# New states of the sample group updated in place, with five buffers and steps ten weight units apart, in a hybrid recurrent decoder step

## The chip, the cores and the metric

The kernel is one program on one core of a Trainium2 chip. The core has a matrix engine (TensorE, PE), a vector engine (VectorE, DVE), an activation engine (ScalarE, ACT), GpSimd (POOL) and an engine that here only issues transfers (SyncE, SP), and 16 DMA engines between HBM and the on-chip memory. Times are device microseconds (us) of one execution. The measure is the median of several runs.

## The reference: what is computed

One inference step of a decoder layer for 256 prompt tokens and 8 samples that share the weights, 264 columns in all. Three token mixers (RWKV-7, mLSTM, gated linear attention) run between one input projection and one output projection; a SwiGLU block follows. Besides the outputs, the new recurrent states are results. For the 8 samples, one token each, the three updates are (cut from the reference):

```python
S = (S * jnp.exp(ld_t)[:, :, None, :]                                  # RWKV-7, per head 64 x 64
     - jnp.einsum('bhvk,bhk->bhv', S, kk_t)[..., None] * (kk_t * a_t)[:, :, None, :]
     + v_t[..., :, None] * k_t[..., None, :])
C = a_c[..., None, None] * C + jnp.einsum('bhs,bhsd,bhse->bhde', w_s, kc, vc)   # mLSTM, 4 heads 256 x 256
S = jnp.exp(bL[:, :, 0, :])[..., None] * S + jnp.einsum('bhsd,bhse->bhde', kc * jnp.exp(bL - b), vc)  # GLA, 4 heads 128 x 256
gg, uu = jnp.split(rmsnorm(x, norm2_g) @ ffn_w_gu, 2, axis=-1)
x = x + (jax.nn.silu(gg) * uu) @ ffn_w_down
```

With one token, each update is "old state times a decay, plus an outer product of a value and a key".

## The kernel before

**The weight stream.** All matrices are stored as one stream of 613 units, most of them 128 x 1024 elements (512 KB). For each unit `weights` loads `raw` (3 buffers) on SP's queue at line 331, ACT rounds it to `wh` (line 334, 3 buffers), DVE subtracts to get the remainder `wl` (line 257, 3 buffers), and PE multiplies: 24 matmuls of 128 x 264 to a unit, three for each 128 x 128 block (`wh` by the input's high part, `wh` by its low part, `wl` by its high part). A `raw` buffer comes free when `wl` of the unit three before it is written, so one turn of the buffers is three units.

**What goes on beside it.** After the products of each half unit's columns `fill` may run a step of other work. The samples' new states are such work: `later` makes 16 jobs `new_C` (mLSTM, two samples of a head to a job), then 16 jobs `new_S` (GLA), then 8 jobs `new_W` (RWKV-7). They are written in the program from the SwiGLU block on; a scheduler decides where they stand on each engine, and it places them from the output projection on, over units 316 to 408 of the stream.

**A job new_C.** It loads `Cb` (the old state, 512 KB, 3 buffers) and `kb` (the key, spread over all partitions, 256 KB, 2 buffers). ACT makes the outer product in `kv` (four instructions, 2 buffers), DVE adds the scaled old state to it (two instructions), SP stores `kv` to `o_sC`.

**A job new_S.** It loads `Sb` and `kgb` (256 KB each); POOL multiplies `Sb` by the decay in `kgb`, ACT makes the outer product in `kvg` (four instructions, buffers shared with `kv`), DVE adds the two, SP stores `kvg` to `o_sg`.

**A job new_W.** It loads `Ss` (256 KB), works on it in place on POOL and DVE, and stores it to `o_swkv`.

Every engine takes its own instructions in order, and SP too: a transfer whose wait is not over holds those behind it. Stores of the states are issued by SP straight behind the instruction that makes them; other stores go through `store`, a list that the next `fill` issues.

Of the kernel before, what the change touches and what calls it, by code (L numbers as in the profile page):

```python
# [16 lines left out]
P = 128  # L17
T = 256
B = 8
# [7 lines left out]
INV = 28  # half-units that the inverse is given  # L27
CT = 6
LAST = 4  # gates left for the change from the mixers to the widening
# [18 lines left out]
def _groups():  # L48
    """The weight stream in the order of its use: (name, matrix, column ranges of 256 in all, K-tile ranges)."""
# [45 lines left out]
def _feat(v):  # L95
    """(..., 128 * n) -> (128, n, ...)"""
    v = np.asarray(v)
    v = v.reshape(v.shape[:-1] + (-1, P))
    return np.ascontiguousarray(np.moveaxis(np.moveaxis(v, -1, 0), -1, 1))


def _pad_r(v):
    """R columns -> 26 tiles of 128, the last half empty"""
    out = np.zeros(v.shape[:-1] + (26 * P,), np.float32)
    out[..., :3264] = v
    return out
# [89 lines left out]
def _rows(s):  # L196
    """(B, head, k, 256) -> (head, 128, B, 2, k): a state with its values on the partitions"""
# [4 lines left out]
def _cols(s):  # L202
    """back from _rows"""
# [22 lines left out]
def _unfeat(v):  # L226
    """(128, n, m) -> (m, 128 * n)"""
# [20 lines left out]
def body(tc, a, stop=None):  # L248
# [21 lines left out]
    with ctx:  # L270
# [10 lines left out]
        # ---------------------------------------------------------------- constants  # L281
# [34 lines left out]
        # ---------------------------------------------------------------- the weight stream  # L316
# [23 lines left out]
        def unit(name, ps, k0, nk, hi, lo, kof=0, soon=True):  # L340
            """the products of one unit of weights"""
# [17 lines left out]
        def project(name, hi, lo, kof=0):  # L359
            """The two output tiles of a group of the stream, in PSUM."""  # L360
# [10 lines left out]
        def store(out, in_):  # L371
            """issued a step after what it stores, so that the queue of loads doesn't wait for it"""
            stores.append((out, in_))

        def fill():
            """between the products of the stream: a step of the mixers, now and then one of the samples'"""
# [19 lines left out]
        def both(*gens):  # L396
            """generators side by side"""
# [5 lines left out]
        def table(last):  # L403
            """ACT's tables for exp and ln, after the last use of others"""
# [4 lines left out]
        def scaled(dst, ps):  # L409
            """a group's two tiles, each token by its norm"""  # L410
# [10 lines left out]
        def csum(o, w, hl):  # L421
            """o = w^T (hi + lo) for a w that float32r holds exactly"""
# [7 lines left out]
        # ---------------------------------------------------------------- scratch in DRAM  # L430
# [11 lines left out]
        # ---------------------------------------------------------------- input norm  # L442
# [7 lines left out]
        def first(k0, nk):  # L450
            """a chunk of x: split with the norm's weight; what the norm divides by comes after the product"""
# [34 lines left out]
        def setup():  # L486
            """what the mixers need a little later"""
# [7 lines left out]
            # the low-rank factors of RWKV, both parts of a split on top of one another  # L495
# [24 lines left out]
        # what the samples leave for later  # L520
# [15 lines left out]
        # ---------------------------------------------------------------- RWKV-7  # L536
# [9 lines left out]
        def shift(j, p, dst, rows=P):  # L546
            """token shift: dst = p + (prev - p) * mu; the row that the next call needs is kept"""
# [8 lines left out]
        def sigmoid(x):  # L556
            """1 / (1 + e) from e = exp(-z), in place"""
# [3 lines left out]
        def stack(i, x):  # L561
            """a low-rank factor's input, split, each part twice"""
# [29 lines left out]
        def r_pre(sts, p, r, k, v):  # L592
            """everything of a pair of heads up to the products of its chunks"""
# [90 lines left out]
        def r_inverse(q, sts):  # L684
            """(I + N)^-1 of the 16-blocks of two pairs, by back substitution, one block on a partition"""
# [37 lines left out]
        def r_post(st):  # L723
            p, A, Nr, X, XT, UV, PR, QKt, W = (st[n] for n in ("p", "A", "Nr", "X", "XT", "UV", "PR", "QKt", "W"))
            # 16-blocks to 32-blocks
# [19 lines left out]
            # 32-blocks to 64  # L745
# [15 lines left out]
            # the chain of chunks  # L761
# [61 lines left out]
        def pipeline(jobs):  # L823
            """a stage of every job under way, the eldest first, and one more job"""
# [10 lines left out]
        def dot(out, x, y):  # L835
            """rows of x by rows of y"""
# [734 lines left out]
```

## Time and profile before

| | |
|---|---|
| median of 3 runs | 2044.55 us (2038.8 to 2045.91) |
| the profiled execution, first to last instruction (span) | 2041.8 us |
| PE busy | 1975.7 us, 97% of the span |
| DVE, ACT, POOL busy | 1338.4, 1041.5, 166.5 us |
| DMA | 414.89 MB, mean 203 GB/s |

The span runs from the first instruction to the last; no other time of that execution is given, so it is compared with the runs as it stands: 2.75 us under their median, and inside them. "Busy" of PE counts pipelined matmuls that lie over one another; whether PE keeps its pace is read from the number of matmuls that a stretch holds.

### The profile page before, as it was taken

To read this page: it belongs to the slowest core of one execution; us is meant where nothing else is said; L and a number is where in the kernel's file an instruction comes from. 1 tells how busy PE (TensorE), PEld (TensorE's weight loads), DVE (VectorE), ACT (ScalarE), POOL (GpSimd) and SP (SyncE) were. 2 spreads that over 40 slices of the span, in tenths; PEclk is the share of its full clock that TensorE was granted. 3 is DMA by queue.
4 is the path that set the end of the run, shared out by engine and by line. 5 is a ranking of instruction groups with operands and counts; after the bars stand their busy time and mean duration, and the time that the engine had idled before them with its cause. 6 is when DMAs were issued, how large, how long until landed. Compare 5 with 4: busy or idle time off the path is not lost.

```text
span 2041.8 us, 41005 instructions
## 1 busy us (share of the span) xinstructions
PE 1975.7 (97%) x16526; PEld 1924.8 (94%) x16526; DVE 1338.4 (66%) x2382; ACT 1041.5 (51%) x1700; POOL 166.5 (8%) x257
## 2 busy tenths in 40 slices
PE   8899999999999889999999999999999999999997
PEld 7898999999998888989999998889999999999997
DVE  7776776776775788776566666568754455555554
ACT  5855655655654345556433566554443344444443
POOL 5100100100100321110000000023000000000000
PEclk9999999999999999999999999999999999999999
DMA  8553554564563778658777798888655555555564
GB/s 255 178 182 117 172 178 127 168 174 135 171 174 111 232 254 278 215 170 256 227 227 229 257 311 295 296 297 279 217 176 184 178 186 181 182 184 178 179 183 136
DMA packets 173526, 414.89 MB, mean 203 GB/s; under 512 B 47512, under 2 KB 69432, under 8 KB 173336
## 3 DMA queue, kind: packets, MB, share of 16 engines
q1 hardware_dynamic: 172904, 411.53, 63.2%
q8 instruction: 129, 2.11, 0.4%
q10 hardware_dynamic: 432, 0.74, 0.1%
q14 instruction: 61, 0.50, 0.1%
HBM read 379.61 MB, written 32.61 MB: 202 GB/s over the span
## 4 chain that ended last, share of the span: by engine, by line
PE 70%; DMA 11%; DVE 8%; ACT 6%; issue 3%; SPq 1%; POOL 0%; DVEq 0%; ACTq 0%; POOLq 0%
PE ps L266 63%; PE mx L266 6%; DMA o_sC<-kv 4%; DVE wl L257 4%; ACT wh L334 3%; DMA kgb<-rg_d 2%; DMA of<-o_d 1%; DMA raw<-wst 1%; DVE dot L838 1%; DMA Ss<-wkv 1%; ACT kvg L263 0%; ACT sg L263 0%; ACT kv L263 0%; SPq L331 0%; DVE xl L260 0%
## 5 line engine op out<-in xcount | busy, mean ns | idle before, releaser
L257 DVE TENSOR_TENSOR wl<-raw,wh 128x1024 fp32r<-128x1024 f32 (+2 forms) x613 | 749.1, 1224 | 459.7 <-ACT wh L334 455.3
L334 ACT CAST wh<-raw 128x1024 fp32r<-128x1024 f32 (+2 forms) x613 | 632.2, 1033 | 621.7 <-PE ps L266 542.7
L266 PE MATMUL ps<-xh,wh 128*128 128x264 f32 x2080 | 612.8, 295 | 9.9 <-ACT wh L334 9.8
L266 PE MATMUL ps<-xh,wl 128*128 128x264 f32 x2080 | 598.2, 288 | 14.2 <-DVE wl L257 14.1
L266 PE MATMUL ps<-xl,wh 128*128 128x264 f32 x2080 | 597.3, 287 | 0.0
L266 PE MATMUL ps<-gh,wl 128*128 128x264 f32 x1408 | 402.2, 286 | 13.1 <-DVE wl L257 12.9
L266 PEld LDWEIGHTS ps<-xh,wh 128*128 128x128 f32 x2080 | 397.2, 191 | 18.3 <-ACT wh L334 10.5
L266 PEld LDWEIGHTS ps<-xh,wl 128*128 128x128 f32 x2080 | 396.1, 190 | 18.6 <-DVE wl L257 17.6
L266 PE MATMUL ps<-gh,wh 128*128 128x264 f32 x1408 | 400.9, 285 | 1.7 <-ACT wh L334 1.5
L266 PE MATMUL ps<-gl,wh 128*128 128x264 f32 x1408 | 399.5, 284 | 0.0
L266 PEld LDWEIGHTS ps<-xl,wh 128*128 128x128 f32 x2080 | 397.6, 191 | 1.3
L266 PEld LDWEIGHTS ps<-gh,wl 128*128 128x128 f32 x1408 | 264.5, 188 | 18.4 <-DVE wl L257 18.1
L266 PEld LDWEIGHTS ps<-gh,wh 128*128 128x128 f32 x1408 | 265.0, 188 | 2.8 <-ACT wh L334 2.5
L266 PEld LDWEIGHTS ps<-gl,wh 128*128 128x128 f32 x1408 | 265.1, 188 | 0.0
L266 PE MATMUL ps<-al,wh 128*128 128x264 f32 x704 | 200.5, 285 | 0.0
L266 PE MATMUL ps<-ah,wh 128*128 128x264 f32 x704 | 200.2, 284 | 0.0
L266 PE MATMUL ps<-ah,wl 128*128 128x264 f32 x704 | 199.8, 284 | 0.0
L266 PEld LDWEIGHTS ps<-ah,wl 128*128 128x128 f32 x704 | 133.1, 189 | 0.0
L266 PEld LDWEIGHTS ps<-al,wh 128*128 128x128 f32 x704 | 132.2, 188 | 0.0
L266 PEld LDWEIGHTS ps<-ah,wh 128*128 128x128 f32 x704 | 132.2, 188 | 0.0
L266 PE MATMUL ps<-oh,wh 128*128 128x264 f32 x384 | 109.0, 284 | 0.0
L266 PE MATMUL ps<-oh,wl 128*128 128x264 f32 x384 | 109.0, 284 | 0.0
(406 smaller groups left out, 2382.0 us busy)
## 6 DMA issues: line engine op xcount, KB each, us to landing
raw<-wst SPq DMA_DIRECT2D x579, 512.0 KB, 3.5
raw<-wst SPq DMA_DIRECT2D x32, 384.0 KB, 3.2
Ct<-mC SPq DMA_DIRECT2D x16, 512.0 KB, 5.1
Cb<-mC SPq DMA_DIRECT2D x16, 512.0 KB, 6.7
o_sC<-kv SPq DMA_DIRECT2D x16, 512.0 KB, 6.4
g_d<-sgate SPq DMA_DIRECT2D x24, 264.0 KB, 4.3
sgl<-g_d SPq DMA_DIRECT2D x24, 264.0 KB, 4.0
qb<-rq_d SPq DMA_DIRECT2D x4, 1024.0 KB
```

Source lines behind the costliest of these rows:

```text
L257: vec.tensor_tensor(out=out, in0=x, in1=y, op=op)
L266: pe.matmul(out, lhsT=lhsT, rhs=rhs, start=start, stop=stop)
L334: act.copy(out=wh[:, 0:nk, :], in_=raw[:, 0:nk, :])
L838: vec.tensor_tensor_reduce(out=tm[:, 0:x.shape[1]], in0=x, in1=y, scale=1.0, scalar=0.0, op0=MUL, op1=ADD, accum_out=out)
```

## The change

The three updates work in the tile that holds the old state, all three kinds share five buffers (tag `st`), the key tiles have three instead of two, the stores go through the list `store` instead of straight to SP, and `every[0]` goes from 4 to 10, so a step of this work is written after every tenth `fill` instead of every fourth. In `new_C` ACT scales the old state (two instructions of 512 columns) and DVE adds the outer product (four of 256); in `new_S` POOL's product stays, ACT has nothing to do, and DVE adds the outer product (four of 128).

```diff
         def new_C(h, b):
-            Cb = fp.tile([P, 2, 2, 256], F32, name="Cb", bufs=3)
+            Cb = fp.tile([P, 2, 2, 256], F32, tag="st", name="Cb", bufs=5)
             load(Cb, a["mC"][h, :, b:b + 2])
-            kb = fp.tile([P, 2, 256], F32, name="kb", bufs=2)
+            kb = fp.tile([P, 2, 256], F32, tag="kb", name="kb", bufs=3)
             load(kb, row(rk_d, BW * b + 256 * h, [[BW, 2], [1, 256]]))
             yield
-            kv = fp.tile([P, 2, 2, 256], F32, name="kv", bufs=2)
+            for i in range(2):
+                af(Cb[:, i], Cb[:, i], AF.Identity, scale=scS[:, h, b + i:b + i + 1])
+            yield
             for i in range(2):
                 for j in range(2):
-                    af(kv[:, i, j, :], kb[:, i, :], AF.Identity, scale=vS[:, 0, 2 * h + j, b + i:b + i + 1])
-            yield
-            for i in range(2):
-                if i:
-                    yield
-                stt(kv[:, i], Cb[:, i], scS[:, h, b + i:b + i + 1], kv[:, i], MUL, ADD)
-            nc.sync.dma_start(out=a["o_sC"][h, :, b:b + 2], in_=kv)
+                    stt(Cb[:, i, j, :], kb[:, i, :], vS[:, 0, 2 * h + j, b + i:b + i + 1], Cb[:, i, j, :], MUL, ADD)
+            store(a["o_sC"][h, :, b:b + 2], Cb)

         def new_S(h, b):
-            Sb = fp.tile([P, 2, 2, P], F32, name="Sb", bufs=3)
+            Sb = fp.tile([P, 2, 2, P], F32, tag="st", name="Sb", bufs=5)
...
-            kv = fp.tile([P, 2, 2, P], F32, tag="kv", name="kvg", bufs=2)
             pool.tensor_tensor(out=Sb, in0=Sb, in1=kb[:, :, 1:2, :].to_broadcast([P, 2, 2, P]), op=MUL)
+            yield
             for i in range(2):
                 for j in range(2):
-                    af(kv[:, i, j, :], kb[:, i, 0, :], AF.Identity, scale=vS[:, 1, 2 * h + j, b + i:b + i + 1])
-            yield
-            tt(kv, kv, Sb, ADD)
-            nc.sync.dma_start(out=a["o_sg"][h, :, b:b + 2], in_=kv)
+                    stt(Sb[:, i, j, :], kb[:, i, 0, :], vS[:, 1, 2 * h + j, b + i:b + i + 1], Sb[:, i, j, :], MUL, ADD)
+            store(a["o_sg"][h, :, b:b + 2], Sb)

         def new_W(v0):
-            S = fp.tile([P, 8, 64], F32, tag="Sb", name="Ss", bufs=3)
+            S = fp.tile([P, 8, 64], F32, tag="st", name="Ss", bufs=5)
...
-            nc.sync.dma_start(out=a["o_swkv"][:, v0:v0 + 8, :], in_=S)
+            store(a["o_swkv"][:, v0:v0 + 8, :], S)
...
-        every[0] = 4
+        every[0] = 10
...
-        while bg:
+        while bg or stores:
             fill()
```

Where the instructions stand moves less than the number ten suggests: the state loads stand between the same weight units as before (the first `Cb` behind unit 316 in both, the first `Sb` behind 364 and now 366, the last `Ss` behind 403 and now 401).

**First place: SP and ACT, late in the new_C jobs.** SP before; the numbers name tiles, in the order in which they are made:

```order
L331 DMA raw_16287<-wst 128x1024
L369 DMA kb_16819<-rk_d_98 128x2x256
L1469 DMA o_sC<-kv_16740 128x1024
L331 DMA raw_16317<-wst 128x1024
L331 DMA raw_16369<-wst 128x1024
L369 DMA Cb_16899<-mC 128x1024
L331 DMA raw_16399<-wst 128x1024
L369 DMA kb_16901<-rk_d_98 128x2x256
L1469 DMA o_sC<-kv_16812 128x1024
```

and ACT before, at the same place; `kv_16894` takes the buffer that `kv_16740` had:

```order
L334 CAST wh_16246<-raw_16245 128x1024
L263 ACTIVATE kv_16894<-kb_16819,vS_459 128x256
L334 CAST wh_16288<-raw_16287 128x1024
L1527 ACTIVATE sil_16208<-gut_16205 128x264
L263 ACTIVATE kv_16894<-kb_16819,vS_459 128x256 x3
```

SP now:

```order
L331 DMA raw_16267<-wst 128x1024
L369 DMA Cb_18244<-mC 128x1024
L331 DMA raw_16307<-wst 128x1024
L331 DMA raw_16347<-wst 128x1024
L369 DMA kb_18246<-rk_d_98 128x2x256
L379 DMA o_sC<-Cb_17902 128x1024
L331 DMA raw_16378<-wst 128x1024
L369 DMA Cb_18425<-mC 128x1024
```

and ACT now:

```order
L427 CAST ah_15757<-sil_16169 128x264
L334 CAST wh_16268<-raw_16267 128x1024
L263 ACTIVATE Cb_18244<-Cb_18244,scS_458 128x512 x2
L334 CAST wh_16308<-raw_16307 128x1024
L334 CAST wh_16348<-raw_16347 128x1024
```

Before, ACT's `kv_16894` stands ahead of the rounding of `raw_16287`, and it needs the buffer that is stored by a transfer issued behind `raw_16287`. Now ACT's instruction on the state waits for the load `Cb_18244`, issued behind `raw_16267`, and stands behind the rounding of `raw_16267`; in 10 of the 16 jobs one or both of the two stand one unit earlier, as the store's user did before.

**Second place: DVE at the same jobs.** Before:

```order
L257 TENSOR_TENSOR wl_16289<-raw_16287,wh_16288 128x1024
L257 TENSOR_TENSOR sil_16208<-sil_16208,gut_16205 128x264
L260 SCALAR_TENSOR_TENSOR kv_16894<-Cb_16817,scS_458,kv_16894 128x512
L257 TENSOR_TENSOR al_15758<-sil_16208,ah_15757 128x264
L260 SCALAR_TENSOR_TENSOR kv_16894<-Cb_16817,scS_458,kv_16894 128x512
L257 TENSOR_TENSOR wl_16319<-raw_16317,wh_16318 128x1024
L257 TENSOR_TENSOR wl_16371<-raw_16369,wh_16370 128x1024
```

and now:

```order
L257 TENSOR_TENSOR wl_16269<-raw_16267,wh_16268 128x1024
L260 SCALAR_TENSOR_TENSOR Cb_18244<-kb_18246,vS_459,Cb_18244 128x256
L257 TENSOR_TENSOR wl_16309<-raw_16307,wh_16308 128x1024
L260 SCALAR_TENSOR_TENSOR Cb_18244<-kb_18246,vS_459,Cb_18244 128x256 x3
L257 TENSOR_TENSOR wl_16349<-raw_16347,wh_16348 128x1024
```

The load `kb_18246` is issued behind `raw_16347`, and DVE's first use of it now stands ahead of `wl_16309`, the unit before `raw_16347`. That is so in 11 of the 16 jobs; in the other 5 the first use stands behind that unit. Before, it was ACT that used the key: in 10 jobs behind the rounding of the very unit that the load followed, in 6 ahead of it.

**Third place: DVE and SP in the new_S jobs.** SP and DVE before:

```order
L331 DMA raw_17126<-wst 128x1024
L369 DMA Sb_17790<-gS 128x512
L369 DMA kgb_17792<-rg_d_99 128x2x256
L1484 DMA o_sg<-kvg_17784 128x512
L331 DMA raw_17156<-wst 128x1024
```

```order
L257 TENSOR_TENSOR wl_17085<-raw_17083,wh_17084 128x1024
L257 TENSOR_TENSOR kvg_17856<-kvg_17856,Sb_17790 128x512
L257 TENSOR_TENSOR wl_17128<-raw_17126,wh_17127 128x1024
L257 TENSOR_TENSOR wl_17158<-raw_17156,wh_17157 128x1024
L257 TENSOR_TENSOR gut_17116<-ps_16983,rs2_15894 128x264
```

and now:

```order
L331 DMA raw_17001<-wst 128x1024
L369 DMA kgb_19990<-rg_d_99 128x2x256
L379 DMA o_sg<-Sb_19678 128x512
L331 DMA raw_17041<-wst 128x1024
L369 DMA Sb_20140<-gS 128x512
```

```order
L257 TENSOR_TENSOR wl_16963<-raw_16961,wh_16962 128x1024
L260 SCALAR_TENSOR_TENSOR Sb_19988<-kgb_19990,vS_459,Sb_19988 128x128 x4
L257 TENSOR_TENSOR wl_17003<-raw_17001,wh_17002 128x1024
L260 SCALAR_TENSOR_TENSOR Sb_20140<-kgb_20142,vS_459,Sb_20140 128x128 x4
L257 TENSOR_TENSOR wl_17043<-raw_17041,wh_17042 128x1024
```

Both times DVE's use of a job (`kvg_17856` there, `Sb_19988` here) stands ahead of the `wl` of the unit behind which its key is loaded (`raw_17126`, `raw_17001`). The store has moved one unit later.

## Rows read from the trace of the kernel before

**Rows 1.** The page, part 1: busy time, share of the span, instructions.
```profile
PE 1975.7 (97%) x16526; PEld 1924.8 (94%) x16526; DVE 1338.4 (66%) x2382; ACT 1041.5 (51%) x1700; POOL 166.5 (8%) x257
```

**Rows 2.** Busy time by stretch (from:to, length, engines with instruction counts, clock, DMA).
```profile
1140.00:1180.00 40.00, 40.00 (x332) 40.00 (x331) 25.84 (x37) 24.00 (x44) 0.00 (x0) 1.00 0.91 299
1180.00:1305.00 125.00, 117.64 (x927) 113.60 (x926) 81.01 (x113) 74.56 (x133) 0.00 (x0) 1.00 0.90 302
1305.00:1400.00 95.00, 87.99 (x700) 85.35 (x699) 58.75 (x75) 53.99 (x110) 25.57 (x18) 1.00 0.91 297
1400.00:1440.00 40.00, 37.37 (x297) 36.17 (x296) 39.83 (x55) 14.27 (x17) 14.17 (x6) 1.00 0.76 256
```

**Rows 3.** Waits, 1130 to 1440 us: who for whom, total, times, longest.
```profile
ACT kv L263 <- DMA o_sC<-kv: 40.3, 13, 5.2
...
ACT kvg L263 <- DMA kgb<-rg_d: 28.2, 14, 4.3
DVE kvg L257 <- POOL Sb L1478: 26.0, 12, 4.1
...
ACT kv L263 <- DMA kb<-rk_d: 2.6, 2, 2.3
```

**Rows 4.** Timeline of SP, ACT and DVE over one turn of new_C.
```profile
1246.67 0.33 SPq L331 DMA_DIRECT2D raw<-wst  x1
1247.05 0.42 SPq L1469 DMA_DIRECT2D o_sC<-kv  x1
...
1253.59 1.31 ACT L263 ACTIVATE kv<-kb,vS 128x256 f32<-128x256 f32 x3 [4.29 <-DMA o_sC<-kv]
1254.80 1.03 ACT L334 CAST wh<-raw 128x1024 fp32r<-128x1024 f32 x1
...
1255.87 1.23 DVE L257 TENSOR_TENSOR wl<-raw,wh 128x1024 fp32r<-128x1024 f32 x1 [0.58 <-ACT wh L334]
...
1257.12 0.33 SPq L331 DMA_DIRECT2D raw<-wst  x1
```

**Rows 5.** DMA issues, 1140 to 1440 us: size, median us to landing.
```profile
raw<-wst SPq DMA_DIRECT2D x93, 512.0 KB, 5.4
Cb<-mC SPq DMA_DIRECT2D x16, 512.0 KB, 6.7
o_sC<-kv SPq DMA_DIRECT2D x16, 512.0 KB, 6.4
kb<-rk_d SPq DMA_DIRECT2D x16, 256.0 KB, 6.5
```

**Rows 6.** The tile kb: its loads' time to landing.
```profile
DMA to landing us min/median/max: 5.2/6.5/8.9
```

**Rows 7.** DVE's groups by form: busy us, mean ns.
```profile
L260 DVE SCALAR_TENSOR_TENSOR kv<-Cb,scS,kv 128x512 f32<-128x512 f32 x32 | 23.4, 747 | 25.3 <-ACT kv L263 25.2
...
L260 DVE SCALAR_TENSOR_TENSOR o<-o,vecs,bon 128x256 f32<-128x256 f32 x8 | 3.6, 477 | 0.0
...
L260 DVE SCALAR_TENSOR_TENSOR y<-natR,sc,y 128x64 f32<-128x64 f32 x1 | 0.3, 285 | 0.0
```

**Rows 8.** Timeline of SP, POOL and DVE in two new_S jobs.
```profile
1338.44 0.38 SPq L369 DMA_DIRECT2D kgb<-rg_d  x1
...
1339.23 1.29 POOL L1478 TENSOR_TENSOR Sb<-Sb,kgb 128x512 f32<-128x512 f32 x1 [4.17 <-DMA kgb<-rg_d]
...
1341.39 1.23 DVE L257 TENSOR_TENSOR wl<-raw,wh 128x1024 fp32r<-128x1024 f32 x1
...
1344.86 1.29 POOL L1478 TENSOR_TENSOR Sb<-Sb,kgb 128x512 f32<-128x512 f32 x1 [4.33 <-DMA kgb<-rg_d]
...
1346.19 0.69 DVE L257 TENSOR_TENSOR kvg<-kvg,Sb 128x512 f32<-128x512 f32 x1 [3.22 <-POOL Sb L1478]
...
1347.68 1.22 DVE L257 TENSOR_TENSOR wl<-raw,wh 128x1024 fp32r<-128x1024 f32 x1
```

**Rows 9.** SP's own waits, 1130 to 1440 us.
```profile
SPq L369 <- DMA o_swkv<-Ss: 9.9, 5, 2.9
```

More of the change, by code (lines that the diff above doesn't have):

```diff
@@ L1461, in new_C, with new_S @@
+            yield
             for i in range(2):
                 for j in range(2):
-                    af(kv[:, i, j, :], kb[:, i, :], AF.Identity, scale=vS[:, 0, 2 * h + j, b + i:b + i + 1])
+                    stt(Cb[:, i, j, :], kb[:, i, :], vS[:, 0, 2 * h + j, b + i:b + i + 1], Cb[:, i, j, :], MUL, ADD)
+            store(a["o_sC"][h, :, b:b + 2], Cb)
+        def new_S(h, b):
+            Sb = fp.tile([P, 2, 2, P], F32, tag="st", name="Sb", bufs=5)
+            load(Sb, a["gS"][h, :, b:b + 2])
+            kb = fp.tile([P, 2, 2, P], F32, tag="kb", name="kgb", bufs=3)
+            load(kb, row(rg_d, 1536 * b + 384 * h + 128, [[1536, 2], [1, 256]]))
+            yield
+            pool.tensor_tensor(out=Sb, in0=Sb, in1=kb[:, :, 1:2, :].to_broadcast([P, 2, 2, P]), op=MUL)
@@ L1464, in new_C @@
             yield
             for i in range(2):
-                if i:
-                    yield
-                stt(kv[:, i], Cb[:, i], scS[:, h, b + i:b + i + 1], kv[:, i], MUL, ADD)
-            nc.sync.dma_start(out=a["o_sC"][h, :, b:b + 2], in_=kv)
-        def new_S(h, b):
-            Sb = fp.tile([P, 2, 2, P], F32, name="Sb", bufs=3)
-            load(Sb, a["gS"][h, :, b:b + 2])
-            kb = fp.tile([P, 2, 2, P], F32, tag="kb", name="kgb", bufs=2)
-            load(kb, row(rg_d, 1536 * b + 384 * h + 128, [[1536, 2], [1, 256]]))
-            yield
-            kv = fp.tile([P, 2, 2, P], F32, tag="kv", name="kvg", bufs=2)
-            pool.tensor_tensor(out=Sb, in0=Sb, in1=kb[:, :, 1:2, :].to_broadcast([P, 2, 2, P]), op=MUL)
-            for i in range(2):
@@ L1496, in new_W @@
             yield
-            tm = fp.tile([P, 8, 64], F32, tag="kb", name="tms", bufs=2)
+            tm = fp.tile([P, 8, 64], F32, tag="kb", name="tms", bufs=3)
             pool.tensor_tensor(out=tm, in0=along(5), in1=col(uR), op=MUL)
```

## The prediction

> **What bounds the kernel now.** The page comes first. PE is busy for 97% of the span [rows 1], so the only time to be won is where PE loses its pace, and busy time hides that, because matmuls lie over one another. The count of matmuls by stretch shows it. From 1140 to 1180 us there are 332 in 40 us, 0.1205 us each, as in undisturbed stretches; a weight unit of 24 then takes 2.89 us and a turn of the three `raw` buffers 8.67 us. By that pace the 927 matmuls of 1180 to 1305 need 111.7 us of the 125, the 700 of 1305 to 1400 need 84.4 of the 95, and the 297 of 1400 to 1440 need 35.8 of the 40 [rows 2]. So 13.3, 10.6 and 4.2 us are lost, 28 us in all, and these three stretches are the jobs new_C, new_S and new_W. That is 1.4% of the kernel, and more than that the change cannot win. The clock is at its full level in all of them, and the DMA engines are 0.90, 0.91 and 0.76 busy [rows 2].
>
> Next come the waits, which say who makes PE late. ACT stood 40.3 us, 13 times, until a store `o_sC` had landed, 28.2 us for `kgb`, and only 2.6 us for `kb`; DVE stood 26.0 us for POOL's `Sb` [rows 3]. ACT and DVE make `wh` and `wl`, so every such wait stands in front of the weights.
>
> The timeline of one turn shows the loop in new_C. `raw` is issued at 1246.67, the store behind it at 1247.05; ACT may write `kv` again only at 1253.59, then rounds that `raw` at 1254.80, DVE makes `wl` at 1255.87, and that frees the buffer for the `raw` at 1257.12 [rows 4]. One turn took 10.45 us against 8.67. The loss of 1.78, 13 times, would be 23 us; PE lost 13.3, because the weights made ahead absorb the rest. I take that share, 0.57, as what a lengthening of this loop costs PE.
>
> **The change, part by part.**
>
> *new_C, ACT.* The wait for the store goes: no tile is written while its store is under way, unless it is the fifth before. In its place ACT waits for the load `Cb`, at the same depth in 10 of 16 jobs and one unit later in the others, as the order shows. The nearest rows for the two prices are the transfers themselves: the store lands after 6.4 us, the load after 6.7 [rows 5]. So the turn through ACT stays about as long. The Trainium skill (DMA: Bandwidth & Descriptors, section on the anatomy of one DMA) says that the receipt of the write makes most of a transfer's fixed cost, and that HBM as the target is the heaviest case; by it the wait taken away would be longer than the one put in. The rows don't bear that out, since the store into HBM is the shorter by 0.3 us; by the rule new_C would gain, which is a rival below.
>
> *new_C, DVE.* This is new. In 11 of 16 jobs DVE's first use of `kb` stands one unit deeper than the load's own unit, so two `wl` wait for a load that was issued behind the later of their two `raw`. The turn is then: 0.38 from `raw` to the next issue (as 1246.67 to 1247.05), the landing of `kb`, one instruction of 256 columns, a `wl`, three more, a `wl`. A `scalar_tensor_tensor` of 256 columns takes 0.477 us [rows 7], a `wl` 1.23 [rows 4], so it is 0.38 + 0.48 + 1.23 + 1.43 + 1.23 = 4.75 plus the landing. With the median of 6.5 it is 11.25, with the least, 5.2, it is 9.95 [rows 6]. In the other 5 jobs all four stand before one `wl`: 0.38 + 1.91 + 1.23 = 3.5 plus the landing, 10.0 or 8.7. Against 8.67, the 16 jobs cost 11 x 2.58 + 5 x 1.33 = 35 us with the median, and 11 x 1.28 + 0 = 14 with the least. PE's share of 0.57 makes 20 and 8, where 13.3 is lost now: +7 or -5. If nothing is absorbed, the upper end is 35 - 13 = +22. I take the median, since it is this same load behind the same neighbours, and a little off it for a stretch that is less crowded when it is longer: **+6 us**, kept between -5 and +22. The part on ACT runs beside it and isn't added.
>
> *new_C, work.* Two instructions of 512 columns at 0.747 us become four of 256 at 0.477: 1.91 for 1.49 a job [rows 7], 6.6 us of DVE over 16 jobs, already inside the turn. The Trainium skill (VectorE: DVE Perf Modes, section on the TRN2 errata) says that each instruction pays a fixed cost and that tiles of 512 elements or more should be used, which speaks against this cut. Its fixed 58 cycles at 0.96 GHz would be 0.06 us an instruction, an estimate by that page, 2 us over the 32 added ones. The rows agree in direction and make it larger: 2 x 0.477 - 0.747 = 0.21 us.
>
> *new_S.* ACT's four instructions go, and its wait of 28.2 us [rows 3] with them. But DVE waits for POOL at the same depth as before, as the third place in the order shows, and the chain ends on DVE. From POOL's start to the start of `wl` it is now 1341.39 - 1339.23 = 2.16 us, and 1347.68 - 1344.86 = 2.82 in the next job, where other work lies between [rows 8]. Afterwards it is POOL's 1.29 plus four instructions of 128 columns. Between 0.285 for 64 and 0.477 for 256 [rows 7] the straight line gives 0.349, four make 1.40, where `kvg` takes 0.69 [rows 8]. The sum is 2.69, 0.5 longer than the one and 0.1 shorter than the other: on the mean +0.2, 16 times 3.2, PE's share **+2 us**. Bounds: 16 x 0.53 = +8 on one side; on the other, if ACT's wait was the true holder in half of the jobs, half of the 10.6 comes back, -5.
>
> *new_W.* The arithmetic stays. SP's wait of 9.9 us until a store of `Ss` lands [rows 9] goes, since five buffers stand where three stood. But DVE is busy for 39.83 of these 40 us [rows 2], and earlier loads don't shorten that. **-1 us**, between -4.2, all that is lost, and 0.
>
> *Stores a step later, spacing of ten.* The order shows stores zero to two units later and the jobs over the same units; a later store delays no load, as the fifth buffer is still free. Zero, hidden by the `raw` waits that SP has anyway. Were the jobs spread in truth, the DMA share of 0.9 would fall; the order says that they are not.
>
> **The sum.** 6 + 2 - 1 = +7 us on the profiled 2041.8, or 2048.8. The runs' median stands 2.75 above that span, so I forecast **2051 us**, 0.3% slower. Of this kernel a difference of about 0.5%, 10 us, is what a measurement can tell from none; the forecast lies inside it.
>
> **The rivals.**
>
> *Faster: the store was the true holder.* If a load that ACT waits for is there in time, because nothing but a free buffer holds it, the 40.3 us of waits vanish. For it: the store's wait is the longest of all on ACT and `kb` cost ACT only 2.6 us [rows 3]. Against it: the order has the loads no earlier. Three quarters of new_C's loss come back, -10, with -3 each from new_S and new_W: 2044.55 - 16 = 2028.5. This is also how it would go by the Trainium skill's rule on write receipts.
>
> *Slower: the key's load on DVE isn't absorbed.* PE waits for `wl`, and `wl` stands behind `kb` two deep; with the lead used up, the full +22 falls due, and +8 in new_S: 2044.55 + 30 = 2074.5. It decides from a landing of about 6 us at a share near one. For it: the loop is closed in 11 jobs, one after another. Against it: the present loop was not charged in full either.
>
> *No difference: the DMA engines set the pace.* At 0.90 busy [rows 2] the same bytes may need the same time whoever waits: 2044.5. For it, the share; against it, stretches nearly a tenth idle, with waits by turns.
>
> **How the numbers follow.** The forecast, -4 to +14 around 2051, has 0.47, the faster rival 0.20, the slower 0.18, the pace of the DMA 0.15. From 2030 to 2068 about 8 in 10 is held: beyond lie half of the faster rival and a little less than half of the slower. Without the rivals the range is 2040 to 2059. Slower by over 0.5% are most of the slower rival (0.16) and the upper part of the forecast (0.15), 0.31; faster 0.20, nearly all the faster rival; within it 0.49.
>
> **What would show it.** No wait of ACT for `o_sC`; in its place one for `Cb` of some 2 to 3 us a job. DVE waiting for `kb`, 20 us or more in all. Four instructions of 0.48 and 0.35 us. ACT without waits in new_S, DVE's wait for POOL still near 26 us. Some 33 us of PE's pace lost over the three stretches instead of 28. The forecast is wrong if `kb` lands before DVE comes to it, if new_C's turn stays under 9.5 us, or if the lost matmuls are found elsewhere than here.

## The result and the profile after

The changed kernel takes 2051.64 us in the median of 6 runs (2048.97 to 2055.62), the kernel before 2042.08 us on the same chip (6 runs, 2038.8 to 2045.91). The ratio is 1.0051, 95% interval 1.0037 to 1.0065: slower by half a per cent, and no run lies on the other side. Differences in us below are a ratio less one, times 2044, so this one is +10.4. The profiled execution has a span of 2053.9 us; that is at the upper end of its six runs, and the one of before [rows 1] lies in the middle of its own.

PE is as busy as before, and just as little is to be read from it (the page, part 1; compare [rows 1]):

```profile
PE 1975.8 (96%) x16526; PEld 1926.9 (94%) x16526; DVE 1345.1 (65%) x2462; ACT 1017.9 (50%) x1604; POOL 167.7 (8%) x257
```

The number of matmuls by stretch tells it. The same four stretches are taken for both kernels, the last one their sum. First the kernel before (busy time by stretch; PE, PEld, DVE, ACT, POOL with instruction counts, clock, DMA share, GB/s):

```profile
1140.00:1310.00 170.00, 162.64 (x1297) 158.60 (x1296) 110.30 (x154) 101.20 (x178) 0.00 (x0) 1.00 0.90 301
1310.00:1410.00 100.00, 91.88 (x728) 88.88 (x728) 65.26 (x83) 55.41 (x109) 27.26 (x20) 1.00 0.89 293
1410.00:1460.00 50.00, 48.48 (x391) 47.57 (x391) 44.66 (x61) 20.32 (x26) 12.47 (x5) 1.00 0.75 246
1140.00:1460.00 320.00, 302.99 (x2412) 295.06 (x2411) 220.22 (x297) 176.94 (x313) 39.73 (x24) 1.00 0.87 290
```

and the changed kernel:

```profile
1140.00:1310.00 170.00, 156.61 (x1260) 153.45 (x1259) 110.47 (x183) 94.81 (x145) 0.00 (x0) 1.00 0.88 295
1310.00:1410.00 100.00, 85.11 (x673) 83.11 (x672) 59.99 (x117) 33.55 (x41) 26.61 (x18) 0.98 0.85 272
1410.00:1460.00 50.00, 46.86 (x372) 45.37 (x371) 48.42 (x68) 19.34 (x24) 13.88 (x6) 1.00 0.78 255
1140.00:1460.00 320.00, 288.58 (x2300) 281.94 (x2298) 218.88 (x365) 147.69 (x210) 40.49 (x24) 0.99 0.86 281
```

At 0.1205 us a matmul, 2412 need 290.6 of the 320 us and 2300 need 277.2. So 29.4 us were lost before and 42.8 are lost now, 13.4 more, where the spans differ by 12.1: the whole difference is here. By stretch it is 18.2 for 13.7 (mostly new_C), 18.9 for 12.3 (mostly new_S) and 5.2 for 2.9. The count in 320 us, a matmul at 0.1205 us, is the measure for every run below.

The stretches are fixed in time, and a kernel that has fallen behind has other work in them. So the matmul records of the same executions were also counted by weight unit (24 to a full unit). From the first matmul of unit 300 to that of unit 364 (new_C) PE takes 199.5 us before and 204.0 now, from there to unit 396 (new_S) 105.1 and 113.9, from there to unit 412 (new_W) 49.3 and 49.7. Behind that both take 565.3 us, and the changed kernel reaches unit 300 1.5 us earlier.

The waits of the changed kernel, 1130 to 1460 us (who for whom; total us, times, longest), against [rows 3]:

```profile
ACT wh L334 <- DMA raw<-wst: 56.6, 37, 3.6
POOL Sb L1475 <- DMA kgb<-rg_d: 56.1, 11, 7.6
...
DVE Sb L260 <- POOL Sb L1475: 37.9, 14, 5.6
...
ACT Cb L263 <- DMA Cb<-mC: 32.2, 11, 5.4
...
DVE Cb L260 <- DMA kb<-rk_d: 28.2, 13, 4.5
```

ACT's 40.3 us for the store and 28.2 for `kgb` [rows 3] are gone. ACT now waits 32.2 us for the load `Cb`, DVE 28.2 us for `kb`, for which nobody waited long before, and DVE's wait for POOL has grown from 26.0 to 37.9. ACT also waits 56.6 us for `raw`. That is no sign of a loss by itself: in the run `late_all` below it waits 73.3 us for `raw`, and PE keeps its pace there in new_C.

The transfers, 1140 to 1440 us (size, median us to landing), against [rows 5]; 88 loads of `raw` stand where there were 93:

```profile
raw<-wst SPq DMA_DIRECT2D x88, 512.0 KB, 5.1
Cb<-mC SPq DMA_DIRECT2D x16, 512.0 KB, 7.8
o_sC<-Cb SPq DMA_DIRECT2D x16, 512.0 KB, 6.3
kb<-rk_d SPq DMA_DIRECT2D x16, 256.0 KB, 6.3
```

One turn of new_C (timeline of SP, ACT and DVE; in brackets the idle time before and what ended it), to be laid beside [rows 4]:

```profile
1275.85 0.43 SPq L369 DMA_DIRECT2D kb<-rk_d  x1
...
1275.84 0.72 ACT L263 ACTIVATE Cb<-Cb,scS 128x512 f32<-128x512 f32 x1 [5.42 <-DMA Cb<-mC]
...
1281.30 0.49 DVE L260 SCALAR_TENSOR_TENSOR Cb<-kb,vS,Cb 128x256 f32<-128x256 f32 x1 [2.53 <-DMA kb<-rk_d]
1281.70 1.22 DVE L257 TENSOR_TENSOR wl<-raw,wh 128x1024 fp32r<-128x1024 f32 x1
...
1284.30 1.22 DVE L257 TENSOR_TENSOR wl<-raw,wh 128x1024 fp32r<-128x1024 f32 x1
...
1285.93 0.43 SPq L369 DMA_DIRECT2D kb<-rk_d  x1
```

DVE stands until `kb` is there, 5.45 us after its issue, then makes one product, a `wl`, the rest and the second `wl`; both `raw` wait for these, and the next `kb` is issued 10.08 us after the first. This is the loop that the prediction drew: 4.63 us beside the landing, where it had 4.75.

In new_S (timeline of POOL and DVE; [rows 8] before):

```profile
1364.47 1.26 POOL L1475 TENSOR_TENSOR Sb<-Sb,kgb 128x512 f32<-128x512 f32 x1 [6.58 <-DMA kgb<-rg_d]
1365.76 1.14 DVE L260 SCALAR_TENSOR_TENSOR Sb<-kgb,vS,Sb 128x128 f32<-128x128 f32 x4 [5.57 <-POOL Sb L1475]
1366.82 1.22 DVE L257 TENSOR_TENSOR wl<-raw,wh 128x1024 fp32r<-128x1024 f32 x1
```

From POOL's start to `wl` it is 2.35 us, between the 2.16 and 2.82 of [rows 8], but DVE has stood for 5.57 us ahead of that `wl`. The row shows a second thing: the four instructions take 1.14 us together, less than four times the 0.35 us that one lasts, because each begins before the one ahead of it has ended.

### The profile page after: what moved, and what is told of

Read it like the earlier page. It is cut to its first block, busy times and chain, and to the rows that moved or that the text cites. A ratio compares the mean times of both kernels' runs of the same rounds, so it can differ in the third digit from the quotient of the medians.

```text
span 2053.9 us, 40965 instructions
## 1 busy us (share of the span) xinstructions
PE 1975.8 (96%) x16526; PEld 1926.9 (94%) x16526; DVE 1345.1 (65%) x2462; ACT 1017.9 (50%) x1604; POOL 167.7 (8%) x257
## 4 chain that ended last, share of the span: by engine, by line
PE 73%; DVE 10%; DMA 8%; ACT 4%; issue 3%; SPq 1%; POOL 1%; DVEq 0%; ACTq 0%; POOLq 0%
PE ps L266 66%; PE mx L266 6%; DVE wl L257 4%; DMA raw<-wst 3%; ACT wh L334 2%; DMA kb<-rk_d 2%; DMA kgb<-rg_d 2%; DVE dot L838 1%; DMA Cb<-mC 1%; DVE Cb L260 1%; POOL Sb L1475 0%; DVE Ss L257 0%; DVE Sb L260 0%; DMA St<-gS 0%; SPq L331 0%
```

## The experiments

Each kernel was timed in five rounds against the kernel before on the same chip (`spacing_only` in three). Matmuls in 1140 to 1460 us, and PE's time by weight units, come from each kernel's profiled execution, which is one execution and not the median.

| run | ratio, 95% interval | us | matmuls | lost, us | units 300 to 364, us | 364 to 396 | 396 to 412 |
|---|---|---|---|---|---|---|---|
| before | 1 | 0 | 2412 | 29.4 | 199.5 | 105.1 | 49.3 |
| changed | 1.0051 (1.0037 to 1.0065) | +10.4 | 2300 | 42.8 | 204.0 | 113.9 | 49.7 |
| spacing_only | 1.0008 (0.9995 to 1.0021) | +1.6 | 2403 | 30.4 | 197.7 | 107.2 | 50.2 |
| c_only | 1.0032 (1.0019 to 1.0045) | +6.5 | 2360 | 35.6 | 203.7 | 107.6 | 48.9 |
| s_only | 1.0018 (1.0008 to 1.0029) | +3.7 | 2378 | 33.5 | 198.2 | 109.6 | 50.3 |
| stores_now | 1.0021 (1.0007 to 1.0035) | +4.3 | 2370 | 34.4 | 200.5 | 108.8 | 49.7 |
| old_math_in_place | 0.9988 (0.9975 to 1.0001) | -2.5 | 2436 | 26.5 | 195.8 | 105.8 | 49.5 |
| late_use | 1.0021 (1.001 to 1.0032) | +4.3 | 2398 | 31.0 | 197.8 | 108.1 | 49.7 |
| late_s | 0.9978 (0.9967 to 0.9989) | -4.5 | 2447 | 25.1 | 204.6 | 94.3 | 50.9 |
| late_all | 0.9883 (0.987 to 0.9897) | -23.9 | 2587 | 8.3 | 186.8 | 95.1 | 50.9 |
| late_before | 0.9933 (0.9921 to 0.9945) | -13.7 | 2557 | 11.9 | 186.8 | 98.2 | 51.4 |
| spread10 | 0.987 (0.9851 to 0.9889) | -26.6 | 2592 | 7.7 | 187.1 | 98.0 | 47.1 |
| spread_after10 | 0.9908 (0.9893 to 0.9923) | -18.8 | 2588 | 8.1 | 188.8 | 94.4 | 48.8 |
| spread_late | 0.9849 (0.9836 to 0.9861) | -30.9 | 2640 | 1.9 | 186.8 | 93.0 | 46.5 |

The column of lost time, less 29.4, agrees with the third column to within 5 us in every row, to within 3 in most; in the three spread kernels part of the jobs lies behind the window, and behind these units. `spread_late` loses next to nothing, so its row serves as the full pace below. The same work ahead of unit 300 took between 1104.1 and 1113.4 us in the fourteen executions; a median carries that too, the last three columns don't.

### Which part of the change: spacing_only, c_only, s_only

`spacing_only` is the kernel before with one number changed:

```diff
-        every[0] = 4
+        every[0] = 10
```

> The kernel before with the spacing of ten alone. Every engine's instructions stand in the same order as before, so by the theory of the prediction (what counts is where the instructions stand, and the scheduler, not the spacing, sets that) it takes the time of before, ratio 1.000 within 0.003. A rival by which the spacing itself moves the work would give a share of the 9.6 us.

Nothing measurable: the order of the instructions is, row for row, that of before, because the scheduler places the jobs over the same units whatever the distance in the program.

`c_only` is the changed kernel with new_S computed as before (`kvg` on ACT, one sum on DVE, its store issued at once); `s_only` is the changed kernel with new_C as before, spacing of ten kept, with four buffers `st` and two for the keys:

```diff
 c_only, new_S
-                    stt(Sb[:, i, j, :], kb[:, i, 0, :], vS[:, 1, 2 * h + j, b + i:b + i + 1], Sb[:, i, j, :], MUL, ADD)
-            store(a["o_sg"][h, :, b:b + 2], Sb)
+                    af(kv[:, i, j, :], kb[:, i, 0, :], AF.Identity, scale=vS[:, 1, 2 * h + j, b + i:b + i + 1])
+            yield
+            tt(kv, kv, Sb, ADD)
+            nc.sync.dma_start(out=a["o_sg"][h, :, b:b + 2], in_=kv)
 s_only, new_C
-                af(Cb[:, i], Cb[:, i], AF.Identity, scale=scS[:, h, b + i:b + i + 1])
+                for j in range(2):
+                    af(kv[:, i, j, :], kb[:, i, :], AF.Identity, scale=vS[:, 0, 2 * h + j, b + i:b + i + 1])
...
-                    stt(Cb[:, i, j, :], kb[:, i, :], vS[:, 0, 2 * h + j, b + i:b + i + 1], Cb[:, i, j, :], MUL, ADD)
-            store(a["o_sC"][h, :, b:b + 2], Cb)
+                stt(kv[:, i], Cb[:, i], scS[:, h, b + i:b + i + 1], kv[:, i], MUL, ADD)
+            nc.sync.dma_start(out=a["o_sC"][h, :, b:b + 2], in_=kv)
```

> The changed kernel with new_S as before (product on ACT in kvg, one addition on DVE, store issued at once). By the sum of the prediction new_C makes most of the loss: about 6 us slower than before, 2048. By a reading of the changed kernel's trace, in which new_S loses more per weight unit than new_C, it is only 2 to 4 us slower, 2045. If the key's wait on DVE cost nothing, it is at 2042 or below.

> The changed kernel with new_C as before (kv, ACT's four products, store issued at once). By the sum of the prediction new_S and new_W together cost 1 us, 2043. By a reading of the changed kernel's trace it is 6 to 8 us, 2049, since DVE's four instructions behind POOL, and POOL's waits, lengthen each turn.

+6.5 and +3.7 us; together 10.2 of 10.4. The first is what the prediction's sum gave; the second lies between its two expectations. Two thirds come with new_C, one third with new_S. new_W is changed in both runs, and its units take 48.9 and 50.3 us for 49.3, so it adds little to either. The profiled execution of the changed kernel divides otherwise, 4.5 us in new_C and 8.8 in new_S; it lies 4.0 us over its kernel's median, and in new_S it has 4.3 us more than `s_only`. The waits of `c_only` are those of the changed kernel in new_C:

```profile
ACT Cb L263 <- DMA Cb<-mC: 33.3, 12, 4.5
DVE Cb L260 <- DMA kb<-rk_d: 30.5, 14, 4.6
```

and in `s_only` DVE's wait for POOL is again longer than the 26.0 of [rows 3]:

```profile
DVE Sb L260 <- POOL Sb L1477: 32.6, 15, 4.1
```

### The stores: stores_now

The changed kernel, its stores issued by SP straight behind the instruction (the same edit for `o_sg` and `o_swkv`):

```diff
-            store(a["o_sC"][h, :, b:b + 2], Cb)
+            nc.sync.dma_start(out=a["o_sC"][h, :, b:b + 2], in_=Cb)
```

> The changed kernel with its stores issued by SP straight behind the instruction that makes the state, no longer by the next step. The prediction put the later store at zero: 2048 to 2054, ratio to before about 1.005. If a store straight behind the sum holds SP until DVE is done, and the next raw with it, it is slower: 2055 to 2065. If a later store is itself the cost, because it lands among the next loads, it falls to 2042.

It came out 0.3% under the changed kernel, some 6 us, and the two intervals don't overlap; that is under the first expectation's ratio of 1.005, and not down to the third's 2042. But more moved than the stores: in this kernel's order DVE's first use of the key stands one unit deeper than the load's unit in 8 jobs, in the changed kernel in 11. The wait for the key shows it, 13.2 us where there were 28.2:

```profile
DVE Cb L260 <- DMA kb<-rk_d: 13.2, 8, 3.3
```

By the prediction's own prices, 2.58 us a turn for a deep job and 1.33 for a shallow one, three such jobs are some 4 us of turns. So most of the gain can be had from the places alone; whether the later transfer costs anything by itself stays open.

### Was the store the true holder: old_math_in_place

The arithmetic of before, but the sum is written into the old state's tile (four buffers `st`), so that no `kv` waits for a store:

```diff
-                stt(kv[:, i], Cb[:, i], scS[:, h, b + i:b + i + 1], kv[:, i], MUL, ADD)
-            nc.sync.dma_start(out=a["o_sC"][h, :, b:b + 2], in_=kv)
+                stt(Cb[:, i], Cb[:, i], scS[:, h, b + i:b + i + 1], kv[:, i], MUL, ADD)
+            nc.sync.dma_start(out=a["o_sC"][h, :, b:b + 2], in_=Cb)
...
-            tt(kv, kv, Sb, ADD)
+            tt(Sb, kv, Sb, ADD)
```

> The kernel before, its arithmetic and immediate stores kept, but DVE writes the sum into the tile of the old state (four shared buffers), so ACT's product tile is free before the store lands: ACT's wait for o_sC goes and nothing is moved to DVE. If that wait was the true holder of new_C (the faster rival of the prediction), it is 6 to 12 us faster than before; by the theory that ACT then waits for the key at the same place, it is within 4 us of before.

The waits of this run:

```profile
ACT kvg L263 <- DMA kgb<-rg_d: 31.2, 16, 4.0
ACT kv L263 <- DMA kb<-rk_d: 30.5, 14, 4.1
```

The 40.3 us for the store are gone, and the same instruction waits 30.5 us for the key, where it had waited 2.6 [rows 3]. The gain is 2.5 us, with no change just inside the interval, as the second expectation had it. Behind the store stood a load that was nearly as late. It was not only there already: with the buffer free earlier, the scheduler also puts ACT's first use of the key ahead of the rounding of the unit that the key's load follows in 15 of 16 jobs, where it did so in 6 before. So this run doesn't price the store's wait alone; `late_before` below does better.

### The place of the use: late_use, late_s, late_all, late_before

Same arithmetic, same buffers, loads behind the same units or within one of them, as in the changed kernel; only the instruction that uses a load is ordered behind the weights of the unit behind which the load is issued. It is an order, no wait. In `late_use` this holds for DVE's use of `kb`, in `late_s` for DVE's instructions of new_S, in `late_all` for both and for ACT's scaling of `Cb`:

```diff
+        def behind(i, last):
+            dep = mybir.DependencyInfo(mybir.DependencyClass.NoSync, mybir.DependencyReason.DATA)
+            tc.add_manual_dep(i.ins, last.ins.name, dep, reason="order")
...
-                    stt(Cb[:, i, j, :], kb[:, i, :], vS[:, 0, 2 * h + j, b + i:b + i + 1], Cb[:, i, j, :], MUL, ADD)
+                    o = vec.scalar_tensor_tensor(out=Cb[:, i, j, :], in0=kb[:, i, :], scalar=vS[:, 0, 2 * h + j, b + i:b + i + 1],
+                                                 in1=Cb[:, i, j, :], op0=MUL, op1=ADD)
+                    behind(o, wls[KB[4 * h + b // 2] - 1])
```

> The changed kernel with DVE's use of the key in new_C moved behind the wl of the weight unit that its load follows, one or two units later than now; loads, stores and the amount of work are the same. Theory (a wait for a load that stands ahead of the weights makes PE late): DVE's 28 us of waits for kb fall under 8, and the kernel gets 4 to 8 us faster than the changed one, about 2045. If the DMA engines set the pace, or DVE's larger number of instructions, nothing changes: 2051.6 within 3.

DVE's wait for the key has left the list, and 6.1 us of the 10.4 are back, as expected; but ACT's wait has grown from 32.2 to 40.1. In part its place has moved: the scheduler now puts ACT's scaling ahead of its load's unit in 14 jobs, where it was 10:

```profile
ACT Cb L263 <- DMA Cb<-mC: 40.1, 16, 4.6
```

> The changed kernel with only new_S's DVE instructions ordered behind the wl of the unit behind which their key is loaded; new_C as the change has it. Moving DVE's use of the key in new_C was worth 6 us, moving all three kinds of use 31 us, so ACT's scaling and new_S share the other 25. If each of these waits costs by the stretch in which it stands, new_S holds what PE lost there, 18.9 us by the windows of the changed kernel, and new_S alone gives back 10 to 17: 2035 to 2042, ratio to before about 0.997. If the waits of new_S are only charged because PE comes out of new_C with no weights made ahead, it gives back less than 5: about 2048.

The first theory: 14.9 us under the changed kernel, and the windows put it where it was done, 808 matmuls for 673 in the second stretch, 16.3 us (by weight unit 94.3 us for 113.9). In the first there is no gain, 1254 for 1260, and every use in new_C stands where it stood, so weights made ahead are not what new_S lacked:

```profile
1140.00:1310.00 170.00, 157.76 (x1254) 154.58 (x1254) 110.10 (x183) 94.25 (x144) 0.00 (x0) 0.99 0.89 291
1310.00:1410.00 100.00, 98.69 (x808) 97.97 (x807) 84.99 (x138) 40.48 (x50) 39.33 (x21) 1.00 0.95 323
```

> As late_use, and also ACT's scaling of Cb in new_C and DVE's four instructions in new_S stand behind the weight unit that their load follows. Theory: these are the other waits ahead of the weights, so ACT's wait for Cb (32 us) and DVE's wait for POOL (38 us) shrink by more than half and the kernel comes to or below the kernel before, ratio 0.996 to 1.000. If the DMA engines set the pace it stays where late_use is, 1.002.

34.3 us under the changed kernel, and 23.9 under the one before, far more than the expectation, which ended at the kernel before. The two waits it names are down from 32.2 and 37.9 us:

```profile
ACT Cb L1473 <- DMA Cb<-mC: 5.5, 6, 1.8
DVE Sb L1493 <- POOL Sb L1489: 6.5, 5, 1.9
```

Its windows:

```profile
1140.00:1310.00 170.00, 170.00 (x1402) 169.94 (x1401) 124.65 (x204) 104.25 (x154) 5.39 (x4) 1.00 0.95 329
1310.00:1410.00 100.00, 96.58 (x778) 94.69 (x778) 87.94 (x141) 39.77 (x49) 41.64 (x20) 1.00 0.92 304
```

1402 matmuls at 0.1205 are 168.9 of 170 us: PE keeps its pace through all of new_C, with the DMA engines 0.95 busy at 329 GB/s, more than in either kernel. 6.1 and 14.9 being the key's and new_S's part, 13.3 are left for ACT's scaling, by subtraction; it wasn't run alone, and since `late_use` moved it too, this is a remainder and not its price.

`late_before` does the same to the kernel before: its products on ACT and, in new_S, its sum on DVE go behind the unit of their load; arithmetic, buffers and `every[0] = 4` stay.

```diff
-                    af(kv[:, i, j, :], kb[:, i, :], AF.Identity, scale=vS[:, 0, 2 * h + j, b + i:b + i + 1])
+                    o = act.activation(out=kv[:, i, j, :], in_=kb[:, i, :], func=AF.Identity, scale=vS[:, 0, 2 * h + j, b + i:b + i + 1])
+                    behind(o, whs[KV[4 * h + b // 2] - 1])
```

> The kernel before, its arithmetic, buffers, stores and dense placement kept, with ACT's products and DVE's sum of new_S ordered behind the rounding (the remainder) of the unit behind which their key is loaded. If the place of the use is what costs and not the arithmetic, it comes to where the changed kernel with its late uses came: 2016 to 2026, ratio 0.987 to 0.991. If two tiles kv make ACT wait for o_sC as before, since that wait is not moved behind a load, the 40 us on ACT stay in new_C and only new_S gains: 2030 to 2038.

2029.57 us, 13.7 under the kernel before: just past the second theory's range and short of the first's. The second theory's reason fell all the same. The store's wait, which was not touched, fell from 40.3 us to 2.5, and the wait for the key is gone too. The order shows why: behind its key's unit, ACT's first product also stands behind the unit that the store is issued behind, in 13 of the 14 jobs that wait for one. The store's wait, then, was of the same kind as the loads':

```profile
ACT kvg L1491 <- DMA kgb<-rg_d: 8.7, 9, 2.1
...
ACT kv L1472 <- DMA o_sC<-kv: 2.5, 2, 2.3
```

new_C runs at full pace here as well, 1401 matmuls in the first stretch:

```profile
1140.00:1310.00 170.00, 170.00 (x1401) 169.94 (x1401) 122.58 (x168) 111.76 (x196) 3.91 (x3) 1.00 0.94 328
1310.00:1410.00 100.00, 95.47 (x770) 93.59 (x769) 76.77 (x96) 54.80 (x103) 28.99 (x20) 1.00 0.90 294
```

Its median is 9 us over that of `late_all`, the profiled span 8.5. Of these 8.5, 3.5 lie after new_C, where ACT and DVE still wait for `kgb` and POOL; the other 4.9 lie ahead of unit 300, where neither kernel has a job. Whether the arithmetic has a share in that isn't shown.

### The jobs spread in truth: spread10, spread_after10, spread_late

Each load of a state or a key is ordered behind the weight load written last before it, so the scheduler can't bring it forward, and a distance of ten becomes real. Ten are ten half units, so five weight units and not the ten of the title: the loads `Cb` follow units 343, 348, 353 and so on, and the jobs lie over units 343 to 565. `spread10` has the arithmetic of before, `spread_after10` that of the change.

```diff
+        def late(out, in_):
+            dep = mybir.DependencyInfo(mybir.DependencyClass.NoSync, mybir.DependencyReason.DATA)
+            tc.add_manual_dep(nc.sync.dma_start(out=out, in_=in_).ins, behind[0].ins.name, dep, reason="spread")
...
-            load(Cb, a["mC"][h, :, b:b + 2])
+            late(Cb, a["mC"][h, :, b:b + 2])
```

> The kernel before with a real spacing: each load of a state is ordered behind the load of the weight unit at which the program writes it, and steps are ten fills, so the jobs lie over units 343 to 565 instead of 316 to 408. Theory: most of the 28 us that PE loses come back, since DMA share and landings fall; 15 to 25 us faster than before, ratio 0.988 to 0.993. If waits ahead of the weights count whatever the load, each job still costs its turn and it gains under 8 us.

> The changed kernel with the same real spacing. By the theory the order inside a job matters little once a job has five units to itself: within 4 us of the other spread kernel, 15 to 25 us faster than before. If DVE's wait for the key two units deep costs 2 us a job in any case, it is 10 us or more slower than the other.

Both are far under the kernel before, but the changed arithmetic is here the slower of the two by 7.8 us; it was expected level. What holds it is open. Its waits for `Cb` and `kb` were still there, but in `spread10` ACT also waits 46.3 us for `kb`, and units 300 to 412, with nearly all of new_C, take 332.1 us in the one and 332.0 in the other. Of the 8.4 us between the two profiled spans 4.8 lie ahead of unit 300 and 3.7 behind unit 412. `spread_late` moves these uses too, three to five units behind their loads:

> The changed arithmetic with its jobs spread in truth, ten half units apart, and every use three to five units behind its load. Spread alone gave 2026.6 with this arithmetic and 2018.3 with that of before. If what was left of the waits there (ACT for Cb 39.5 us, DVE for kb 26.7) is what kept it above, it comes to 2012 to 2018 and those waits go. If the bytes beside the weights are charged in any order, it stays at 2018 to 2022, as the late uses in the dense order did.

The fastest of all, 2013.01 us in the median, 1.5% under the kernel before, as the first theory had it. No wait for a load of new_C or new_S is left on ACT or DVE. In 1140 to 1440 us it issues

```profile
raw<-wst SPq DMA_DIRECT2D x103, 512.0 KB, 3.9
```

103 units of the 103.8 that 2.89 us each allow.

## Why the prediction was right, and where

The time, 2051 for 2051.64, and the sign are right, and so is the mechanism in new_C. That the time is met so closely is partly luck: it was built on the 2044.55 us of three runs, where six give 2042.08, and against that the step was larger than forecast, +10.4 for +7. The ratio, 1.0051, lies just in the part over 0.5% that had a chance of 0.31. The steps:

- **The stage and the waits.** All of the difference lies in the three stretches. ACT's wait for the store gave way to one for `Cb`, 32.2 us over 16 jobs, 2.0 a job (forecast 2 to 3). DVE waits 28.2 us for `kb` (20 or more). 42.8 us of pace are lost (41.8 of them in the prediction's 1140 to 1440 us), where some 33 were forecast; that figure was itself low, since its own sum of +7 on 28 makes 35. A part of the rest is this profiled run, at the upper end of its kernel's, the remainder are the terms below.
- **new_C, +6.** `c_only` measured +6.5 (3.9 to 9.2 by its interval). The mechanism is right; that the sum comes out is luck, by two errors that go against each other. First, the present turn: one of 10.45 us was taken for thirteen, and from it the share of 0.57. From the issue of unit 316 to that of unit 364, 16 turns, it is 154.9 us, 9.68 each. Over a stretch that long PE multiplies what is loaded, so its loss follows the mean turn, and no share is absorbed beyond the weights made ahead at the start: the 93 loads of [rows 5] in 300 us give turns of 9.68, 31 us over the pace, of which PE lost 28; the 88 loads now give 10.23 and 45.8 us, of which 42 are lost. Second, the new turn was forecast at 8.67 + 35/16 = 10.86 on the mean; the same 16 turns now take 160.9 us, 10.06 each. The deep one shown above took 10.08, since its key landed after 5.45 us and not 6.5. Both turns were too long by 0.8, and what counts is their difference: 0.38 us, 6.0 in 16 turns.
- **"The part on ACT runs beside it and isn't added."** This step hid the most. The two waits run side by side, and when one alone is taken away the other grows (`late_use`: 6.1 us back, ACT's wait up to 40.1); together with new_S's they hold 34 us.
- **new_S +2 and new_W -1.** `s_only` measured +3.7 (1.6 to 5.9) for both: mis-sized by some 3 us. POOL's start to `wl` was forecast at 2.69 and took 2.35 in the job shown: each of the four instructions lasts the forecast 0.35 us, but they overlap, so that 1.14 us stand for the 1.40 of the sum. What was wrong is that DVE's wait for POOL would stay near 26: it is 32.6 there and 37.9 in the changed kernel. A likely reason, not shown, is that with ACT no longer held DVE comes to the instruction sooner and stands there longer; the 28.2 us of ACT's wait brought nothing, as the step said. That earlier loads give new_W 1 us wasn't seen: units 396 to 412 take 49.7 us for 49.3 (the 5.2 us for 2.9 of the third stretch are mostly work that came later; `spacing_only`, with the order of before, holds 374 matmuls there, the changed kernel 372).
- **Spacing, zero.** Shown (`spacing_only`). **Stores later, zero.** Not shown: with the stores at once 6 us came back, though in an order that also has fewer deep jobs. This division goes across the one by jobs, since both `c_only` and `s_only` have late stores.
- **Faster, the store was the true holder.** Fell: the changed kernel has no such wait and is slower, and `old_math_in_place` takes that wait away and gains 2.5 us, not 16. It was a holder, but one of several of the same kind (`late_before`). By the Trainium skill (DMA: Bandwidth & Descriptors, section on the anatomy of one DMA) the receipt of the write is most of a transfer's fixed cost, and heaviest into HBM, so a store's wait would be the dearer one; the section describes transfers that GpSimd issues, and here SP issues them. The landings don't bear it out: `o_sC` lands after 6.3 us, the load `Cb` of the same size after 7.8.
- **Slower, the key isn't absorbed.** That nothing is absorbed was right; its price of +22 was not, since it needs mean turns of 10.86.
- **No difference, the DMA engines set the pace.** Fell: in `late_all` they are 0.95 busy in new_C and PE loses 1 us in 170.
- **The cut of 512 into 256 columns.** It costs DVE the forecast 0.48 us an instruction, and nothing that PE feels where DVE isn't made to wait (`late_all`, units 300 to 364 at full pace). The fixed cost of which the Trainium skill (VectorE: DVE Perf Modes, section on the TRN2 errata) warns is seen in the rows and isn't on the path.

What bounds new_C, then, is neither the arithmetic nor the buffers nor the bytes, since `late_all` and `late_before` differ in the first two and both take 186.8 us for units 300 to 364; in new_S it is most of the loss. An engine that takes its instructions in order made the weights late because an instruction that needs a transfer stood ahead of a weight that was loaded before that transfer. `late_all` and `late_before` show it with nothing else changed but what the scheduler shifts by a unit. The prediction's ceiling of 28 us for any change here is about right: `late_all` gains 23.9, and `spread_late`, whose jobs lie elsewhere, 30.9 (28.4 to 33.5), a little over it; by its units 300 to 412, 326.3 us for 354.0, it is 27.7.

Open stay: what the later store costs alone; ACT's part of the 34 us by itself; why the changed arithmetic is slower in the spread order and faster in the late one; and the cause of what `late_all` still loses, 6.5 us against full pace. By weight units none of that is in new_C, 2.1 are in new_S, and 4.4 in new_W, whose uses no run of the dense kernels moved. (In the second stretch it holds 778 matmuls where `late_s` has 808, but it is further on in the stream there; for units 364 to 396 the two take 95.1 and 94.3 us.)

## What to carry to other kernels

Where an in-order engine prepares a stream and does side work from the same queue of loads, look for each side instruction at which load it needs and which stream loads were issued ahead of that; put it behind the stream work of those, and the one or two units of delay cost nothing here. When a long wait is removed, ask which transfer would hold the same instruction next, and whether a scheduler now moves that instruction forward: here the next was the key's load, nearly as late as the store. And what a lengthened loop costs is worked out from the mean of its turns over the whole stretch, before and after alike, not from one turn.

## What the runs showed of the hardware

PE's clock fell after PE had stood, though not each time. In the changed kernel PE waited 4.1 us for one `wl` in new_S (windows of 4 us):

```profile
1364.00:1368.00 4.00, 0.03 (x1) 0.00 (x0) 2.24 (x6) 0.00 (x0) 1.26 (x1) 0.95 0.51 176
1368.00:1372.00 4.00, 3.91 (x21) 3.91 (x22) 3.84 (x9) 2.72 (x4) 1.28 (x1) 0.63 0.72 223
```

In the second window the granted clock is 0.63 on the mean, between its levels of 2.4 GHz (1.0) and 1.2 GHz (0.50 from 1367.6 to 1371.0), and it holds 21 matmuls where the next windows hold 35: 1.7 us more beside the wait itself. Two other stands of PE in this stretch, 2.2 us at 1338.8 and 2.0 at 1353.0, were not followed by a dip. A dip in the second stretch is also in the profiled runs of `c_only`, `late_use`, `old_math_in_place` and `spacing_only`, whose order is that of before, so it is no part of the change.

POOL and DVE held each other up. POOL's product of 128 x 512 takes 1.29 us in the median, but longer when it begins while DVE makes a `wl`: 2.23, 2.22 and 1.45 us in three of the changed kernel's 16 jobs, 2.18, 1.89, 1.47 and 1.43 in four before. In all seven it ends 1.14 to 1.16 us after that `wl` has ended, nearly its own whole length, whatever their overlap was. One of them (timeline of POOL and DVE); DVE's next instruction waited for it:

```profile
1355.67 2.22 POOL L1475 TENSOR_TENSOR Sb<-Sb,kgb 128x512 f32<-128x512 f32 x1 [3.40 <-DVE Sb L260]
...
1355.52 1.21 DVE L257 TENSOR_TENSOR wl<-raw,wh 128x1024 fp32r<-128x1024 f32 x1
1357.92 1.14 DVE L260 SCALAR_TENSOR_TENSOR Sb<-kgb,vS,Sb 128x128 f32<-128x128 f32 x4 [1.19 <-POOL Sb L1475]
```

The other way round, a `wl` that DVE began at 1382.46 us, 0.14 us after a product of POOL, took 2.24 us instead of 1.22 and ended 1.08 us after it. In these records the two instructions don't run together: the later one gets on when the earlier is done. No run tried it apart.
